# Last quarter of T4 split straight into its tile, the other three quarters loaded ahead

## Chip, cores and metric

The kernel runs on one core of one Trainium2 chip. The metric is the device time of one execution in microseconds (us); the median of several executions is compared. TensorE is called PE here, its weight loads PEld, VectorE DVE, ScalarE ACT, GpSimd POOL and SyncE SP. POOL and SP also issue DMA transfers, each from its own queue, in program order.

## What is computed

One inference step of a small encoder trunk with one layer: 2048 new frames of a first stream and 32 further frames of a running one, with 1024 channels. The part around the change is the combined input projection of the normed frames:

```python
def layer(h, p, conv_hist, pool_hist, pos, g_mix, w_in, ...):
    hn = rmsnorm(h, g_mix)
    proj = hn @ w_in                                    # (2048 + 32) x 1024 by 1024 x 3072
    hA, bA, cA, zA, vB, zB = jnp.split(proj, [W_A, 2 * W_A, 3 * W_A, 4 * W_A, 4 * W_A + W_B], axis=-1)
    yA, new_conv = short_conv_mixer(hA, bA, cA, zA, ...)
    yB, new_pool = pooling_mixer(vB, zB, ...)
    h = h + jnp.concatenate([yA, yB], axis=-1) @ w_out
    gate = jax.nn.sigmoid(rmsnorm(h, g_ple) @ w_ple_gate)
    return h + (p @ w_ple) * gate, new_conv, new_pool
```

A final RMSNorm closes the trunk. Everything is float32.

## The kernel before

**Products.** A float32 product is made of three passes: each operand is split into a high part (a cast, on ACT) and a low part (the rest, by a subtraction on DVE), and PE multiplies high by high, high by low and low by high. The helper `split` (L80) does both steps; `put` (L420) applies it to a whole piece of a tile. A half product, `half_product` (L642), is 12 matmuls of 128x128 by 128x512: four chunks of the inner size, three passes each.

**Seven instead of eight.** The 2048 frames are cut into blocks of 512 columns, and two blocks form a group (`GROUPS`). For a pair of weight columns and a pair of blocks, a 2x2 product of halves is made from seven half products (as Strassen and Winograd do) instead of eight. For that, seven combinations of the normed frames are needed, each split in two parts and kept in SBUF: 11, 21, T1, T2, T3, 22 and T4. For a group they fill three big slots of two pieces each, and T4 stands in a tile by itself from the pool `w7`, which has one buffer only (`seventh`, L366). `Unit.pair` (L970) makes the seven half products in a fixed order. Its last one, `half_product(X, make("22"), B["T4"], False)`, is the only one that reads T4; its result is the (1, 0) part.

**The first unit.** Group 0 begins with a unit done in plain form (`Unit.plain`, L902): eight half products for each of zb, v, c and h, first on block 0, then on block 1, without combinations. Block 1 is read from `hn[1]`, whose first half, `B0["12"]` (L774), lives in the one buffer of `w7`; the T4 of group 0 comes into the same buffer later. The last reader of `B0["12"]` is the product h of block 1. While the plain unit runs, the generator `second_block` (L777) prepares block 1 between its steps: it loads and norms the frames, turns them (on PE), splits them, and then makes the combinations T1, T2, T3 and T4 of group 0, for four column ranges of 128 (c = 0 to 3), one in each of its last four steps. T1, T2 and T3 are split straight into their pieces (L806 to L808). T4 can't be, since its buffer is still taken by `B0["12"]`: `to_memory` (L543) splits each quarter into a small tile of the pool `xin` (four buffers, shared with the raw frames) and writes it to `p_d["T4"]` in device memory, with a DMA from POOL's queue. After the product h, L940 and L941 allocate `B0["T4"]` and load all of it from memory with one DMA of 2 MB, again from POOL's queue; then the third pair of this unit, zab, goes on (`steps`), and its last half product reads T4. The fourth range (c = 3) is made in the step of `second` right after the product h of block 1, that is, just ahead of the load.

**What sets the order.** Tiles come from pools whose buffers are handed on when the last reader is done; a scheduler of the framework orders the instructions of each engine, and each engine then works in that order. A few instructions are pinned. A later unit's first matmuls, its weights' splits and the loads of its raw weights (`raw_weight`, L573, from SP's queue, ring `raws` of three buffers) are placed between those of the unit before.

Of the kernel before, what the change touches and what calls it, by code (L numbers as in the profile page):

```python
# [9 lines left out]
F32 = mybir.dt.float32  # L10
# [5 lines left out]
P = 128  # L16
# [20 lines left out]
def trunk(ctx, tc, x_p, x_s, c_conv, c_pool, p_p, p_s, g_mix, w_in, conv_w, conv_b, pool_w,  # L37
          pool_scale, w_out, g_ple, w_gate, w_ple, g_fin, y_p, y_s, sc_p, sp_p, sc_s, sp_s):
    nc = tc.nc
# [16 lines left out]
    def bank(name):  # L56
        return ps_m.tile([P, 512], F32, tag="mm", name=name)
# [22 lines left out]
    def split(hi, lo, src, eng=nc.vector, later=False):  # L80
        ins = nc.scalar.copy(hi, src)  # L81
        if later:
            tc.keep_in_program_order(ins)
        eng.tensor_tensor(lo, src, hi.bitcast(F32), op=ALU.subtract)  # L84
        return ins
# [256 lines left out]
    def plain(name, A, W, n, carry, out):  # L342

        X, Y, Z = (bank(f"{c}_{name}") for c in "xyz")
        packed(X, A[0], W["11"], n, True)
        c2 = carry(X, (0, 1))
        packed(Z, A[0], W["T1"], n, True)
        packed(Z, A[1], W["22"], n, False)
        out(Z, c2, (0, 1))
        packed(X, A[1], W["21"], n, False)  # L350
        out(X, None, (0, 0))
# [14 lines left out]
    def seventh(name):  # L366
        return w7.tile([P, 2 * KH * NH], F32R, tag="h", name=name)
# [31 lines left out]
    with ExitStack() as s1:  # L399
# [13 lines left out]
        def piece_of(t, i):  # L413

            return t[:, i * PIECE:(i + 1) * PIECE].rearrange("p (k h n) -> p k h n", k=KH, h=2)
# [4 lines left out]
        def put(piece, src, later=False):  # L420

            split(piece[:, :, 0], piece[:, :, 1], src, later=later)

        def ftile(name):
            return fr.tile([P, KH, P], F32, tag="f", name=name)
# [34 lines left out]
        def x_rows(tb, c):  # L460
            r = tb * NB + c * P
            return x_p[r:r + P]

        def x_load(name, src, queue=nc.sync):

            t, n = ring4(xin, f"xt_{name}"), src.shape[0]
            queue.dma_start(t[:n], src)
            return t, n, f"x{name}"

        def x_stat(x, later=False):  # L470

            t, n, name = x
            return t, n, sumsq(t, n, name, later=later)

        def normal(x):
            xt, n, r = x
            nc.vector.scalar_tensor_tensor(xt[:n], xt[:n], r[:n], g_bc[:n], op0=ALU.mult, op1=ALU.mult)

        def turn(x, half, name, get=tbank, later=False):
            xt, n, _ = x  # L480
            pt = get(name)
            for k in range(KH):
                kk = half * KH + k
                ins = nc.tensor.transpose(pt[:, k * P:k * P + n], xt[:n, kk * P:(kk + 1) * P], ident[:n, :n])
                if later:
                    tc.keep_in_program_order(ins)
            return pt.rearrange("p (k t) -> p k t", k=KH)[:, :, :n]
# [50 lines left out]
        p_d = {q: tc.dram_tile([P, KH, 2, NB], F32, name=f"p_d{q}") for q in NAMES}  # L538

        def staged(name):  # L540
            return xin.tile([P, KH, 2, P], F32R, tag="t", name=name)

        def to_memory(mem, name, src, at, later=False):  # L543
            t = staged(name)
            put(t, src, later)
            nc.gpsimd.dma_start(mem[:, :, :, at:at + P], t.bitcast(F32))
# [37 lines left out]
        def weights(kind, j, name):  # L584

            if first_w:
                return first_w.pop(0)
            raw = raw_weight(kind, j, name)
            out = []
            for half in range(2):  # L590
                out.append(wtile(f"w_{name}_{half}"))
                put(out[-1], raw[:, half * KH:half * KH + KH])
            return out
# [55 lines left out]
        def project(ps, w, tb):  # L649
            x = hn[tb]  # L650
            for half in range(2):
                half_product(ps, w[half], x[half], half == 0, half == 1)
# [36 lines left out]
        B0 = {}  # L689
# [87 lines left out]
        def second_block():  # L777

            spans = [(c, slice(c * P, c * P + P)) for c in range(4)]
            xs = []  # L780
            for c in range(4):
                x = x_stat(x_load(f"1_{c}", x_rows(1, c)))
                normal(x)
                xs.append(x)
                yield
            whole = []
            for c, cs in spans:
                x = xs[c]

                turned = x[0].rearrange("p (k t) -> p k t", k=KC)  # L790
                for half, q in enumerate(("12", "22")):
                    pt = turn(x, half, f"pt1_{c}_{half}", bank)
                    put(B0[q][:, :, :, cs], pt)
                    nc.scalar.copy(turned[:, half * KH:half * KH + KH], pt)
                whole.append((turned[:, :KH], turned[:, KH:]))
                yield
            op = lambda o, a, b, op=ALU.subtract: nc.vector.tensor_tensor(o, a, b, op=op)
            for c, cs in spans:
                p12, p22 = whole[c]
                t1, t3, t2, t4 = (ftile(f"f{t}_1_{c}") for t in range(4))  # L800
                part = lambda q, h: B0[q][:, :, h, cs].bitcast(F32)
                op(t1, p12, part("11", 0))
                op(t3, p22, p12)
                op(t1, t1, part("11", 1))
                op(t2, p22, t1)
                put(B0["T2"][:, :, :, cs], t2)  # L806
                put(B0["T1"][:, :, :, cs], t1)
                put(B0["T3"][:, :, :, cs], t3)  # L808
                op(t4, part("21", 0), t2)
                op(t4, t4, part("21", 1), ALU.add)  # L810
                to_memory(p_d["T4"], f"T4_0_{c}", t4, c * P)
                yield

        second = second_block()


# [19 lines left out]
        class Unit:  # L836
# [65 lines left out]
            def plain(self):  # L902
                tbs, j, tag, zs, V, U, c_s = self.tbs, self.j, self.tag, self.zs, self.V, self.U, self.c_s
                blocks = range(len(tbs))

                first = {}

                def product_of(kind, b, w):
                    if b == 0 and kind in first:
                        return first.pop(kind)  # L910
                    ps = bank(f"{kind}{tag}_{tbs[b]}")
                    project(ps, w, tbs[b])
                    return ps

                wz, wv = weights("zb", j, f"zb{tag}"), weights("v", j, f"v{tag}")
                wc = weights("c", j, f"c{tag}")
                first.update(first_products(dict(zb=wz, v=wv, c=wc)))
                for b in blocks:
                    nc.scalar.activation(self.cols(zs, b), product_of("zb", b, wz), AF.Silu)
                    ps = product_of("v", b, wv)  # L920
                    if b:
                        self.mix(0)
                        next(second)
                    nc.scalar.copy(self.place(V, HV, b), ps)
                    self.pool_block(b)
                    nc.scalar.copy(self.cols(c_s, b), product_of("c", b, wc))
                self.mix(1)
                next(second)

                nc.vector.tensor_copy(U[:, :HU], halo_u[:, :, j])  # L930
                wh = weights("h", j, f"h{tag}")
                for b in blocks:
                    ps = product_of("h", b, wh)
                    nc.vector.tensor_tensor(self.place(U, HU, b), ps, self.cols(c_s, b), op=ALU.mult)
                    self.conv(b)
                    if b == 0:
                        steps = self.pair(*self.third(B0), raw_ring, None, True)
                        next(steps)
                    next(second)
                B0["T4"] = piece_of(seventh("B0_T4"), 0)  # L940
                nc.gpsimd.dma_start(B0["T4"].bitcast(F32), p_d["T4"])  # L941
                p_d["T4"] = tc.dram_tile([P, KH, 2, NB], F32, name="p_dT4b")
                for _ in steps:
                    pass
# [356 lines left out]
    with ExitStack() as s2:  # L1301
# [160 lines left out]
        def short_tile():  # L1462
            plain("ol", short_a, W, last_n, *h_ops([short_x], last_n, "ol", two=True))
# [378 lines left out]
```

## Time and profile before

| what | us |
|---|---|
| time, median of 3 runs | 919.31 |
| lowest and highest of them | 918.29, 919.38 |
| time of the profiled execution | 917.26 |
| its span, from the first to the last instruction | 915.5 |

| engine in the profiled execution | busy us | share of the span |
|---|---|---|
| PEld | 722.7 | 79% |
| DVE | 702.6 | 77% |
| ACT | 460.3 | 50% |
| POOL | 151.6 | 17% |

The span is what the trace shows; 1.76 us of the profiled execution's own time lie around it. The plain unit and the pair zab that follows it lie in the first tenth of the span. The page's granted clock of PE is full throughout (0.999 on the mean). In a row of a timeline stand the start, the time from the start to the end, the engine, the line, the operation with out<-in, the shape and the count; in brackets, the idle time ahead of it and what ended it. Several equal instructions that follow each other make one row. In the profile's rows buffer numbers and digits are left out: `B_T` is T4's tile, `p_dT` the memory of a T combination (T4's, in the rows shown here), `T` one of the small tiles, `B` any piece of a big slot or the buffer of `B0["12"]`.

### The profile page before, as it was taken

What the parts mean: (1) busy time and instruction counts of PE and PEld (TensorE: products, weight loads), DVE (VectorE), ACT (ScalarE), POOL (GpSimd) and SP (SyncE); (2) the same over time, 40 slices, a digit from 0 to 9 for tenths busy, and PEclk for the clock granted to TensorE, in tenths of its full rate; (3) what the DMA queues carried; (4) which work ended last, traced back from release to release, by engine and by line L of the source; (5) the groups of instructions that cost most, each with busy time, mean ns of one, the idle gap of its engine ahead of it and who ended that gap; (6) DMA issues with size and microseconds to landing.
All of it is one profiled execution on the core that took longest, in us unless ns stands there. A gap on an engine that the chain in (4) does not pass through costs nothing.

```text
span 915.5 us, 12179 instructions
## 1 busy us (share of the span) xinstructions
PE 895.3 (98%) x4174; PEld 722.7 (79%) x4174; DVE 702.6 (77%) x1158; ACT 460.3 (50%) x834; POOL 151.6 (17%) x291
## 2 busy tenths in 40 slices
PE   8999999999999999999999999999999999999996
PEld 6787888878888877877778887888888788778885
DVE  6897899697894597856667679965576978897885
ACT  7743555555444344533344366544344865565554
POOL 2210121222122104100000020121111211120002
PEclk9999999999999999999999999999999999999999
DMA  8165386749499857577746485787677875575554
GB/s 275 53 186 184 115 239 182 219 147 301 122 313 427 244 161 228 191 231 247 244 132 215 146 310 206 259 235 273 226 258 291 287 256 173 184 234 187 183 187 171
DMA packets 113307, 199.56 MB, mean 218 GB/s; under 512 B 13190, under 2 KB 70062, under 8 KB 112221
## 3 DMA queue, kind: packets, MB, share of 16 engines
q1 hardware_dynamic: 91309, 124.72, 42.3%
q0 software_dynamic: 19488, 69.67, 22.5%
q10 hardware_dynamic: 2448, 4.39, 1.3%
q8 instruction: 33, 0.54, 0.2%
q14 instruction: 29, 0.24, 0.1%
HBM read 133.06 MB, written 65.67 MB: 217 GB/s over the span
## 4 chain that ended last, share of the span: by engine, by line
PE 65%; DMA 7%; issue 5%; DVE 2%; ACT 1%; POOL 1%; SPq 0%; POOLq 0%; DVEq 0%; ACTq 0%
PE x_g L185 9%; PE x_o L185 9%; PE x_zab L646 5%; PE z_g L185 5%; PE e L109 4%; PE x_zbv L646 4%; PE x_ch L646 4%; PE z_o L185 4%; DMA raw_zab_0b<-in_w_in_dram 4%; PE z_zab L646 2%; PE y_g L185 2%; PE y_o L185 2%; PE z_ch L646 2%; PE z_zbv L646 2%; DMA B<-p_d 2%
## 5 line engine op out<-in xcount | busy, mean ns | idle before, releaser
L646 PE MATMUL x_zab<-B,w_zab_S 128*128 128x512 f32 x192 | 46.9, 392 | 0.6 <-ACT V L983 0.4
L185 PE MATMUL z_o<-wo,y_S 128*128 128x512 f32 x192 | 47.4, 389 | 0.0
L185 PE MATMUL z_g<-wg,g_S 128*128 128x512 f32 x192 | 46.8, 391 | 0.0
L646 PE MATMUL z_zab<-B,w_zab_S 128*128 128x512 f32 x192 | 46.7, 390 | 0.0
L185 PE MATMUL x_o<-wo_T,y_S 128*128 128x512 f32 x192 | 46.1, 389 | 0.0
L185 PE MATMUL x_o<-wo,y 128*128 128x512 f32 x192 | 45.2, 389 | 0.0
L646 PEld LDWEIGHTS x_zab<-B,w_zab_S 128*128 128x128 f32 x192 | 35.7, 188 | 9.6 <-ACT V L983 0.8
L185 PEld LDWEIGHTS x_o<-wo,y 128*128 128x128 f32 x192 | 36.1, 188 | 7.7
L646 PEld LDWEIGHTS z_zab<-B,w_zab_S 128*128 128x128 f32 x192 | 35.8, 188 | 7.8 <-DVE w_zab_S L84 0.3
L185 PEld LDWEIGHTS z_o<-wo,y_S 128*128 128x128 f32 x192 | 36.0, 188 | 7.5
L646 PE MATMUL x_ch<-B,w_ch_S 128*128 128x512 f32 x168 | 41.9, 392 | 0.0
L185 PEld LDWEIGHTS x_o<-wo_T,y_S 128*128 128x128 f32 x192 | 36.0, 188 | 7.4
L646 PE MATMUL z_ch<-B,w_ch_S 128*128 128x512 f32 x168 | 40.5, 390 | 1.4 <-ACT U L983 1.4
L185 PEld LDWEIGHTS z_g<-wg,g_S 128*128 128x128 f32 x192 | 35.8, 188 | 7.5 <-ACT c_g L1566 0.2
L646 PE MATMUL x_zbv<-B,w_zbv_S 128*128 128x512 f32 x168 | 40.8, 392 | 0.6 <-ACT zs L983 0.6
L646 PE MATMUL z_zbv<-B,w_zbv_S 128*128 128x512 f32 x168 | 40.4, 390 | 0.0
L646 PEld LDWEIGHTS z_ch<-B,w_ch_S 128*128 128x128 f32 x168 | 31.5, 188 | 8.3 <-ACT U L983 1.8
L646 PEld LDWEIGHTS x_zbv<-B,w_zbv_S 128*128 128x128 f32 x168 | 31.3, 188 | 8.3 <-ACT zs L983 1.0
L646 PEld LDWEIGHTS x_ch<-B,w_ch_S 128*128 128x128 f32 x168 | 31.3, 188 | 7.3 <-issue 0.4
L646 PEld LDWEIGHTS z_zbv<-B,w_zbv_S 128*128 128x128 f32 x168 | 31.5, 188 | 6.5
L81 ACT CAST y_S<-y_fS 128x512 fp32r<-128x512 f32 x28 | 17.0, 620 | 27.2 <-PE x_o L185 11.5
L1316 DVE TENSOR_TENSOR c_o<-x_o,x 128x512 f32<-128x512 f32 x14 | 9.7, 690 | 21.9 <-PE x_o L185 21.8
(550 smaller groups left out, 2289.4 us busy)
## 6 DMA issues: line engine op xcount, KB each, us to landing
wn<-in_w_in_dram SPq DMA_DIRECT2D x24, 512.0 KB, 5.3
p_dT<-T POOLq DMA_DIRECT2D x16, 512.0 KB, 5.4
y<-y_d SPq DMA_DIRECT2D x16, 512.0 KB, 6.5
e<-e_d SPq DMA_DIRECT2D x15, 512.0 KB, 4.5
x<-in_x_prompt_dram SPq DMA_DIRECT2D x14, 512.0 KB, 5.2
B<-p_d POOLq DMA_DIRECT2D x3, 2048.0 KB, 15.7
B<-p_dT POOLq DMA_DIRECT2D x3, 2048.0 KB, 21.6
h_d<-x SPq DMA_DIRECT2D x12, 512.0 KB, 7.2
```

Source lines behind the costliest of these rows:

```text
L81: ins = nc.scalar.copy(hi, src)
L109: nc.tensor.matmul(ps, pps[:, a, k], wp[k][b][:, cs], start=k + q == 0, stop=k == 1 and q == 2)
L185: nc.tensor.matmul(ps[:n], lhs[:, k, a, :n], w[b][:, k], start=start and k + q == 0, stop=k == KH - 1 and q == 2, skip_group_check=True)
L646: nc.tensor.matmul(ps, lhs[:, k, x], b[:, k, y], start=start and k + q == 0, stop=stop and k == KH - 1 and q == 2, skip_group_check=True)
L1316: add = lambda o, a, b: nc.vector.tensor_tensor(o, a, b, op=ALU.add)
```

## The change

Of the four quarters of T4 the first three are still split into small tiles and written to memory. In the step of the fourth, the tile `B0["T4"]` is allocated, one DMA loads the columns of the first three quarters from memory, and the fourth is split straight into its own columns of the tile. The allocation and the whole load after the product h are gone.

```diff
                 op(t4, part("21", 0), t2)
                 op(t4, t4, part("21", 1), ALU.add)
-                to_memory(p_d["T4"], f"T4_0_{c}", t4, c * P)
+                if c < 3:
+                    to_memory(p_d["T4"], f"T4_0_{c}", t4, c * P)
+                else:
+                    B0["T4"] = piece_of(seventh("B0_T4"), 0)
+                    nc.gpsimd.dma_start(B0["T4"][:, :, :, :c * P].bitcast(F32), p_d["T4"][:, :, :, :c * P])
+                    put(B0["T4"][:, :, :, cs], t4)
                 yield
...
                     next(second)
-                B0["T4"] = piece_of(seventh("B0_T4"), 0)
-                nc.gpsimd.dma_start(B0["T4"].bitcast(F32), p_d["T4"])
                 p_d["T4"] = tc.dram_tile([P, KH, 2, NB], F32, name="p_dT4b")
```

In the rows that follow, a name ends with its buffer's number, and digits inside are dropped: `B_T_807` and `B_T_803` are T4's tile, `T_0_0` to `T_0_3` the four small tiles, `p_dT_176` T4's memory. Lines of the changed kernel are up to five higher than before.

On POOL, around the writes of the four quarters, before (the names behind `waits` are counters: `DMASW0` to `DMASW3` count the landings of the four writes, in order):

```order
L546 DMA p_dT_176<-T_0_0_623 1024x1x128 [waits DVE_49]
L546 DMA p_dT_176<-T_0_1_684 1024x1x128 [waits DVE_49]
L546 DMA p_dT_176<-T_0_2_753 1024x1x128 [waits DVE_49]
L546 DMA p_dT_176<-T_0_3_803 1024x1x128 [waits DVE_49]
L941 DMA B_T_807<-p_dT_176 128x4096 [waits DMASW2_49,DMASW1_49,DMASW3_49,DMASW0_49,PE_49]
L73 TENSOR_SCALAR ms_x_3_976<-ssq_x_3_974 128x1 [waits Activation_49]
```

and with the change:

```order
L546 DMA p_dT_176<-T_0_0_623 1024x1x128 [waits DVE_49]
L546 DMA p_dT_176<-T_0_1_684 1024x1x128 [waits DVE_49]
L546 DMA p_dT_176<-T_0_2_753 1024x1x128 [waits DVE_49]
L815 DMA B_T_803<-p_dT_176 128x8x384 [waits DMASW1_49,DMASW2_49,DMASW0_49,PE_49]
L73 TENSOR_SCALAR ms_x_3_974<-ssq_x_3_972 128x1 [waits Activation_49]
```

The fourth write is gone, and the load waits for the three others and for PE (the last matmul that reads `B0["12"]`). It moves 8 runs of 384 elements in each partition where it moved one run of 4096.

On PE, where the pair zab ends and the next unit's first pair, zbv, begins, before (`x_`, `y_` and `z_` are the three accumulators of a pair):

```order
L646 MATMUL x_zab_0_810<-B_2_187,w_zab_0_S_876 128x512 x12
L646 MATMUL z_zab_0_812<-B_2_187,w_zab_0_S_893 128x512 x12
L646 MATMUL x_zbv_1_951<-B_0_185,w_zbv_1_11_954 128x512 x2
L646 MATMUL x_zab_0_810<-B_T_807,w_zab_0_22_913 128x512 x12
L646 MATMUL x_zbv_1_951<-B_0_185,w_zbv_1_11_954 128x512 x10
L646 MATMUL y_zbv_1_952<-B_0_185,w_zbv_1_12_986 128x512 x12
```

and with the change:

```order
L646 MATMUL x_zab_0_808<-B_2_187,w_zab_0_S_874 128x512 x12
L646 MATMUL z_zab_0_810<-B_2_187,w_zab_0_S_891 128x512 x12
L646 MATMUL x_zab_0_808<-B_T_803,w_zab_0_22_911 128x512 x12
L646 MATMUL x_zbv_1_949<-B_0_185,w_zbv_1_11_952 128x512 x12
L646 MATMUL y_zbv_1_950<-B_0_185,w_zbv_1_12_984 128x512 x12
```

Two matmuls of zbv that stood ahead of T4's twelve now stand behind them. It is the only place where PE's order differs.

On ACT, at the cast of the fourth quarter, before:

```order
L81 COPY w_zab_0_S_844<-raw_zab_0a 128x4x128 [waits DVE_49]
L81 COPY w_zab_0_S_860<-s_zab_0_726 128x4x128
L81 COPY T_0_3_803<-f_1_3_790 128x4x128 [waits DMASW1_49,DVE_49]
L983 COPY V_0_334<-x_zab_0_810 128x512 [waits PE_49]
L81 COPY w_zab_0_S_876<-raw_zab_0b 128x4x128 [waits DMAHW5_49]
```

and with the change:

```order
L81 COPY w_zab_0_S_842<-raw_zab_0a 128x4x128 [waits DVE_49]
L81 COPY w_zab_0_S_858<-s_zab_0_726 128x4x128
L81 COPY B_T_803<-f_1_3_790 128x4x128 [waits DVE_49,PE_49]
L986 COPY V_0_334<-x_zab_0_808 128x512 [waits PE_49]
L81 COPY w_zab_0_S_874<-raw_zab_0b 128x4x128 [waits DMAHW5_49]
```

The cast keeps its place; it writes into T4's tile, waits for PE (again the last reader of `B0["12"]`) where it waited for an earlier write's landing, and does not wait for the load. DVE's subtraction for the same quarter keeps its place too. SP's order is unchanged.

## Prediction

> **What bounds the kernel now.** I began with the page's busy times.
>
> ```profile
> span 915.5 us, 12179 instructions
> PE 895.3 (98%) x4174; PEld 722.7 (79%) x4174; DVE 702.6 (77%) x1158; ACT 460.3 (50%) x834; POOL 151.6 (17%) x291
> ```
>
> PE is busy for 895.3 of 915.5 us, so an edit that adds or takes no matmul can win only from the 20.2 us in which PE stands still. Next I read the list of waits, for PE alone over the whole span, because it names these gaps (total us, times, longest).
>
> ```profile
> PE x_zab L646 <- DMA B_T<-p_dT: 2.3, 1, 2.3
> PE e L109 <- DMA wq<-wl_d: 1.6, 1, 1.6
> PE z_ch L646 <- ACT U L983: 1.4, 1, 1.4
> ```
>
> The first is the load that the change touches: once, for 2.3 us. PE's timeline shows the place.
>
> ```profile
> 57.87 11.04 PE L646 MATMUL h<-B,w_h 128*128 128x512 f32 x48
> 82.50 2.88 PE L646 MATMUL z_zab<-B,w_zab_S 128*128 128x512 f32 x12
> 85.22 0.61 PE L646 MATMUL x_zbv<-B,w_zbv 128*128 128x512 f32 x2
> 88.11 2.98 PE L646 MATMUL x_zab<-B_T,w_zab 128*128 128x512 f32 x12 [2.28 <-DMA B_T<-p_dT]
> 90.94 2.43 PE L646 MATMUL x_zbv<-B,w_zbv 128*128 128x512 f32 x10
> 93.20 2.88 PE L646 MATMUL y_zbv<-B,w_zbv 128*128 128x512 f32 x12
> 95.92 2.88 PE L646 MATMUL x_zbv<-B,w_zbv_S 128*128 128x512 f32 x12
> ```
>
> Starts tell the pace: y_zbv begins at 93.20 and the next twelve at 95.92, so twelve matmuls take 2.72 us and one takes 0.227. PE was free for T4's product at 85.22, bridged 0.45 us with two matmuls of the next pair, and stood until 88.11. Why was the load late? POOL's timeline has the writes of the third and fourth quarter and the load, and the DMA part of the trace gives the times from issue to landing (for the stretch from 45 to 95 us, except the last row, which is from the whole span).
>
> ```profile
> 63.36 0.85 POOL L546 DMA_DIRECT2D p_dT<-T  x1 [10.17 <-DVE T L84]
> 73.90 0.85 POOL L546 DMA_DIRECT2D p_dT<-T  x1 [9.69 <-DVE T L84]
> 78.27 0.57 POOL L941 DMA_DIRECT2D B_T<-p_dT  x1 [3.52 <-PE x_zab L646]
> p_dT<-T POOLq DMA_DIRECT2D x4, 512.0 KB, 4.4
> DMA to landing us min/median/max: 3.8/4.4/5.6
> B_T<-p_dT POOLq DMA_DIRECT2D x1, 2048.0 KB, 9.7
> raw_zbv_1a<-in_w_in_dram SPq DMA_DIRECT2D x1, 512.0 KB, 3.8
> raw_ch_1b<-in_w_in_dram SPq DMA_DIRECT2D x1, 512.0 KB, 10.6
> B_T<-p_dT4b POOLq DMA_DIRECT2D x1, 2048.0 KB, 29.3
> ```
>
> The fourth write is issued at 73.90; 78.27 - 73.90 = 4.37 us later, the time of such a write to land, POOL issues the load, and 78.27 + 9.7 = 88.0 is when PE goes on. (The row names PE as releaser; the matmul that the load needs was long done, as worked out below, so it was the write.) The chain is: fourth quarter's split, write, whole load, PE.
>
> **The change, part by part.**
>
> *The load ahead.* It needs three landed writes and the last reader of the buffer. The third write is issued at 63.36; with the 3.8 to 5.6 us that such writes take it has landed between 67.2 and 69.0. The last reader is in the h row: its 48 matmuls start at 57.87, the first 24 belong to block 0, and the next 12 read the buffer, so the 36th ends by 57.87 + 36 x 0.227 + 0.4 = 66.4. The writes end last: issue at up to 69.0. What do the transfer engines do then?
>
> ```profile
> 64.00:68.00 4.00, 4.00 (x19) 3.34 (x18) 4.00 (x8) 1.12 (x2) 0.21 (x1) 1.00 0.83 253
> 68.00:72.00 4.00, 4.00 (x20) 3.23 (x19) 4.00 (x9) 2.10 (x4) 0.00 (x0) 1.00 0.03 9
> 72.00:76.00 4.00, 4.00 (x19) 3.10 (x18) 4.00 (x8) 1.27 (x3) 0.85 (x1) 1.00 0.18 53
> 76.00:80.00 4.00, 4.00 (x19) 3.31 (x18) 4.00 (x9) 3.31 (x7) 0.57 (x1) 1.00 0.46 129
> 80.00:84.00 4.00, 4.00 (x19) 3.33 (x18) 3.95 (x7) 1.81 (x3) 0.00 (x0) 1.00 1.08 406
> 84.00:88.00 4.00, 1.84 (x9) 1.18 (x7) 0.27 (x1) 0.62 (x1) 0.00 (x0) 1.00 1.00 359
> 104.00:108.00 4.00, 4.00 (x24) 3.39 (x22) 2.92 (x6) 1.90 (x4) 0.00 (x0) 1.00 0.00 0
> ```
>
> The columns are the stretch, its length, busy time of PE, PEld, DVE, ACT and POOL with counts, the granted clock, the DMA share and GB/s. From 68 to 76 the engines idle (9 and 53 GB/s, and the latter is mostly the write that goes away), while from 80 to 88, where the load runs now, they are full. The new load moves three quarters of the bytes in shorter runs, a shape that the trace does not show. Its cost is bounded by the nearest rows: below by one load of 512 KB, 3.8 us; above by three quarters of the slowest load of a T4 tile, 0.75 x 29.3 = 22 us. I take three quarters of the same load now, 0.75 x 9.7 = 7.3, because that row shares the buffer and the queue, and it was measured on fuller engines. The load then lands at 69.0 + 7.3 = 76.3, where PE asks at 85.22: 8.9 us to spare. Even three loads of 512 KB at the writes' median, 13.2 us, would land at 82.2.
>
> *PE.* T4's twelve now follow at once, then the other pair's twelve: 85.22 + 2 x 2.72 = 90.66 for the start of y_zbv, where it was 93.20. **The term is -2.54 us**; it holds the gap of 2.28 and some 0.26 of restart. PE's other needs at 85.22 are met: DVE, in its order, has finished all that the product reads before the row at 83.59 below.
>
> *The fourth quarter.* Its cast and subtraction change only their target: nothing on ACT's or DVE's time. The cast gets a wait for PE, and behind it stand on ACT the copy of x_zab's accumulator, for which PE waits, and the next weights.
>
> ```profile
> 71.66 0.61 ACT L81 CAST T<-f 128x512 fp32r<-128x512 f32 x1
> 92.47 0.63 ACT L954 ACTIVATE V<-V 128x512 f32<-128x512 f32 x1 [6.38 <-DVE V L986]
> 93.52 0.58 ACT L983 COPY zs<-x_zbv 128x512 f32<-128x512 f32 x1
> 79.67 0.47 SPq L578 DMA_DIRECT2D raw_ch_1b<-in_w_in_dram  x1
> 83.59 0.68 DVE L84 TENSOR_TENSOR w_zbv_S<-s_zbv,w_zbv_S 128x512 fp32r<-128x512 f32 x1
> 90.41 0.69 DVE L618 TENSOR_TENSOR s_ch<-raw_ch_1b 128x512 f32<-128x512 f32 x1 [6.14 <-DMA raw_ch_1b<-in_w_in_dram]
> 91.75 0.68 DVE L986 TENSOR_TENSOR V<-z_zab,V 128x512 f32<-128x512 f32 x1
> 104.29 0.69 DVE L986 TENSOR_TENSOR V<-x_zbv,V 128x512 f32<-128x512 f32 x1 [0.71 <-PE x_zbv L646]
> ```
>
> The cast runs at 71.66 and its new wait ends by 66.4: nothing, with 5.3 us of cover.
>
> *What was hidden, and is late next.* DVE stands from 84.27 to 90.41 for raw_ch_1b, a raw weight that SP issues at 79.67 into the same crowd: 10.6 us to land, where raw_zbv_1a took 3.8. DVE's wait holds up V<-z_zab, that holds up ACT's silu at 92.47, and behind this, at 93.52, ACT copies x_zbv's accumulator, which PE needs to go on with x_zbv. Today that costs nothing, as the copy ends at 94.1 and PE comes at 95.92. With the change PE comes at 95.92 - 2.54 = 93.38. If raw_ch_1b landed as late as now, PE would wait 0.7 us. But the 2 MB are out of its way: with 3.8 us, or the 5.6 of the slowest write, it lands at 83.5 to 85.3, so about 5 us earlier, and 0.7 us earlier would do. I take nothing, and keep 0.7 for the range.
>
> *Traffic and memory.* One write of 512 KB and a quarter of the load fall away. One small tile fewer moves the ring of `xin` by one place, so some waits name a neighbour's transfer; around 70 us those are writes that have landed by then, and I count nothing.
>
> *After that.* By 104.29 DVE waits for PE again, and from 104 to 108 nothing moves on the DMA engines: whatever was late has been caught up, so everything behind should follow PE, earlier by the same 2.54. The next gap of PE is short.
>
> ```profile
> 140.97 1.06 ACT L94 ACTIVATE junk<-xt 128x1024 bf16<-128x1024 f32 x1 [2.05 <-DMA xt<-in_x_prompt_dram]
> 143.17 3.02 PE L646 MATMUL x_zab<-B,w_zab_S 128*128 128x512 f32 x12 [0.42 <-ACT V L983]
> ```
>
> There ACT waits 2.05 us for frames, and PE for ACT. These loads are released by work that PE paces, so I let the gap stand.
>
> *Sum.* 915.5 - 2.54 = 912.96 for the span, 917.26 - 2.54 = 914.72 for the profiled execution's own time. The median of the runs shown is 2.05 above that execution, so for it 919.31 - 2.54 = **916.8 us**. A measurement of this kernel tells apart about 0.2%, which is 1.84 us.
>
> [...]
>
> **The rivals.**
>
> *A, gain eaten (no change).* Either raw_ch_1b stays late: then 2.54 - 0.7 = 1.84 is left, 917.5. Or later gaps grow, since a load that does not come earlier with PE (the frames at 140.97 are one) gives back what PE gained, up to all of it: 919.3. For it: ACT waits for frames several times. Against it: the idle engines at 104 to 108.
>
> *B, the load ahead is late (slower).* It would sit on POOL's queue or run slowly in its short runs, and PE, which has no two matmuls to bridge with any more, waits for it at 85.22. The new y_zbv starts 5.44 us after the load's landing, against 93.20: it breaks even at 87.8 and costs over 1.84 us from 89.6 on, thus from 20.6 us after an issue at 69.0. At the upper bound of 22 us it lands at 91.0, y_zbv starts at 96.4, 3.2 us later than now: 922.5. [...] For it: B_T<-p_dT4b did take 29.3. Against it: that load was one of seven in a row, this one meets empty engines.
>
> *C, more than the gap.* DVE is 5 us earlier from 84 on, so writes and loads behind it spread, and the gap of 0.42 at 143.17 and half of the 1.4 before z_ch go too: 919.31 - 2.54 - 1.1 = 915.7.
>
> **How the numbers follow.** The forecast as summed gets 0.60, C 0.12, A 0.18, B 0.10. Faster is forecast and C, 0.72; within 0.2% is A, 0.18; slower is B, 0.10. The range reaches below C by the scatter of the runs (about 1 us between 918.29 and 919.38): 914.7; above it takes in A to its end, 919.3. It leaves out B. The likeliest case alone has 916.1 to 917.5.
>
> **What would show it.** Right: PE's row of x_zab<-B_T starts at about 85.2 without a wait; the load is issued at 67 to 69 and lands before 80; DVE's wait for raw_ch_1b is below 2 us; y_zbv starts at 90.7; and PE's busy time is unchanged while its list of waits has lost the first row. The step on the load is wrong if PE still waits there; the step on what is late next, if x_zbv<-B waits for ACT near 93.4; and the step that all behind follows, if the gaps at 143 or 188 have grown by what was won.

## The result, and the profile after

The changed kernel takes 915.72 us (median of 20 runs, 913.53 to 918.41), the kernel before beside it 919.7 (915.68 to 924.4). The ratio is 0.9954, with a 95% interval of 0.9941 to 0.9968: faster by 4.2 us, between 2.9 and 5.4. The forecast was 916.8 by a gain of 2.54 us. The time lies in the range, faster was the likeliest sign, and the gain is larger than its one term; why, is the question of the experiments.

The profiled execution of the changed kernel took 916.19 us, its span is 914.4. PE is busy for 895.2 us (895.3 before). From the list of PE's waits over the whole span (total us, times, longest):

```profile
PE gm L447 <- DMA gm_row<-in_g_mix_dram: 2.3, 1, 2.3
PE e L109 <- DMA wq<-wl_d: 1.5, 2, 0.9
PE z_ch L646 <- ACT U L986: 1.1, 1, 1.1
PE x_zbv L646 <- ACT zs L986: 0.8, 1, 0.8
PE x_zbv L646 <- DVE V L989: 0.7, 1, 0.7
PE x_zab L646 <- ACT V L986: 0.5, 1, 0.5
```

The row of T4's load is gone. Of the rows shown that of 0.7 us for `V` is new; the others were there before within 0.3 us. The timelines of four engines around T4, in the changed kernel:

```profile
57.54 11.04 PE L646 MATMUL h<-B,w_h 128*128 128x512 f32 x48
84.91 2.88 PE L646 MATMUL x_zab<-B_T,w_zab 128*128 128x512 f32 x12
87.63 2.88 PE L646 MATMUL x_zbv<-B,w_zbv 128*128 128x512 f32 x12
90.35 2.88 PE L646 MATMUL y_zbv<-B,w_zbv 128*128 128x512 f32 x12
93.07 2.88 PE L646 MATMUL x_zbv<-B,w_zbv_S 128*128 128x512 f32 x12
67.93 0.92 POOL L815 DMA_DIRECT2D B_T<-p_dT  x1 [4.05 <-DMA p_dT<-T]
85.61 0.69 DVE L618 TENSOR_TENSOR s_ch<-raw_ch_1b 128x512 f32<-128x512 f32 x1 [1.67 <-DMA raw_ch_1b<-in_w_in_dram]
90.55 0.59 ACT L986 COPY zs<-x_zbv 128x512 f32<-128x512 f32 x1 [1.74 <-PE x_zbv L646]
```

T4's twelve start at 84.91 with no wait, and y_zbv, the mark of the prediction, at 90.35 where it was 93.20. That is 2.85 us; but the whole stretch runs 0.33 us earlier in this execution (h starts at 57.54, before at 57.87). From the start of h to that of y_zbv it was 93.20 - 57.87 = 35.33 us and is 90.35 - 57.54 = 32.81: **2.52 us less**, and the forecast's term was 2.54. DVE's wait for raw_ch_1b fell from 6.14 to 1.67, and ACT's copy of x_zbv's accumulator now waits for PE instead of DVE: it ends at 91.14, well before PE comes at 93.07. The landing times, from the DMA part of the trace for 45 to 100 us (count, KB, median us from issue to landing):

```profile
B_T<-p_dT POOLq DMA_DIRECT2D x1, 1536.0 KB, 7.7
raw_ch_1b<-in_w_in_dram SPq DMA_DIRECT2D x1, 512.0 KB, 6.1
```

So near T4 the trace shows what was forecast, and 2.5 us of gain. The two profiled executions, though, are only 1.1 us apart (917.26 and 916.19), while the medians are 4.0 apart. One execution of the kernel before does not tell where its median is.

### The profile page after: what moved, and what is told of

It is laid out like the page before. It is cut to its first block, busy times and chain, and to the rows that moved or that the text cites. A ratio compares the mean times of both kernels' runs of the same rounds, so it can differ in the third digit from the quotient of the medians.

```text
span 914.4 us, 12174 instructions
## 1 busy us (share of the span) xinstructions
PE 895.2 (98%) x4174; PEld 722.6 (79%) x4174; DVE 702.6 (77%) x1158; ACT 460.8 (50%) x834; POOL 149.9 (16%) x290
## 4 chain that ended last, share of the span: by engine, by line
PE 51%; issue 12%; DMA 10%; DVE 3%; POOL 1%; ACT 1%; SPq 0%; POOLq 0%; ACTq 0%; DVEq 0%
PE x_g L185 9%; PE x_o L185 8%; PE z_g L185 5%; PE z_o L185 4%; DMA raw_zab_0b<-in_w_in_dram 4%; PE x_ch L646 3%; PE x_zbv L646 3%; PE x_zab L646 2%; PE y_g L185 2%; PE e L109 2%; PE y_o L185 2%; DMA B<-p_d 2%; PE z_ch L646 1%; PE new L1152 1%; PE z_zab L646 1%
```

## The experiments

### Both kernels again, unchanged

Two theories stood here. G: the length of T4's gap changes from execution to execution, and the profiled one had a short gap. C is the prediction's rival of that letter: the change takes more than the gap, in later waits. The kernel before was profiled three more times, the changed one once more, all on one chip; the expectations call these further profiles the looks.

> The kernel before, unchanged. Theory G (the gap): the measured gain, about 4 us in the medians, is PE's wait for T4's load, and the profiled execution happened to have a short one (2.3 us). Then looks at the kernel before show this wait at different lengths, 2 to 7 us, about 4 us on the mean, and spans that differ by about as much as the waits do. Theory C (the crowd): the wait is always near 2.3 us, and the rest of the gain comes from what the crowd of transfers at 78 to 90 us does elsewhere. Then the waits agree within 0.5 us, and spans above 915.5 are longer at other places.

> The kernel before, unchanged, once more. G: the wait for T4's load between 2 and 7 us, and the span moves with it. C: the wait within 0.5 us of 2.3, and spans move for other reasons.

> The kernel before, unchanged, a third time. G: as in the other looks, the wait and the span move together. C: the wait stays near 2.3 us.

> The changed kernel, unchanged. Both theories: no wait for T4's load, x_zab<-B_T starts within 0.5 us of 85. G: the span lies 2 to 5 us below those of the looks at the kernel before, by what they waited. C: the row of x_zab<-B_T is 2.5 us earlier, and the difference in the spans comes about after 110 us.

They took 922.13, 918.29, 918.73 and 917.98 us. The wait for T4 hardly moves. What moves is the time of the twelve matmuls behind it. PE's timeline in the first further profile of the kernel before:

```profile
87.91 4.57 PE L646 MATMUL x_zab<-B_T,w_zab 128*128 128x512 f32 x12 [2.26 <-DMA B_T<-p_dT]
92.32 2.44 PE L646 MATMUL x_zbv<-B,w_zbv 128*128 128x512 f32 x10
94.60 2.88 PE L646 MATMUL y_zbv<-B,w_zbv 128*128 128x512 f32 x12
```

4.57 us where the first profile had 2.98. The reason stands in the view of windows (stretch, length, busy time of PE, PEld, DVE, ACT and POOL with counts, granted clock, DMA share, GB/s) of the same execution:

```profile
84.00:88.00 4.00, 1.74 (x9) 1.15 (x8) 0.07 (x1) 0.62 (x1) 0.00 (x0) 1.00 1.00 353
88.00:89.00 1.00, 1.00 (x3) 0.80 (x4) 0.00 (x0) 0.00 (x0) 0.00 (x0) 0.55 1.10 356
89.00:90.00 1.00, 1.00 (x3) 0.73 (x3) 0.00 (x0) 0.00 (x0) 0.00 (x0) 0.50 0.17 59
90.00:91.00 1.00, 1.00 (x4) 0.79 (x3) 0.87 (x2) 0.00 (x0) 0.00 (x0) 0.50 0.01 2
91.00:92.00 1.00, 1.00 (x5) 0.83 (x4) 1.00 (x2) 0.00 (x0) 0.00 (x0) 0.75 0.36 137
92.00:93.00 1.00, 1.00 (x6) 0.80 (x5) 0.90 (x3) 0.85 (x2) 0.00 (x0) 1.00 0.98 365
```

The granted clock falls to 0.50 just after PE has gone on and comes back some 3.4 us later. The means of single microseconds tell when: 0.55, 0.51 and 0.85 from 88 to 89 in the three further profiles put the fall 0.2 to 0.6 us after PE's restart (87.91, 87.79, 88.12), and 0.75 and 0.78 from 91 to 92 in the first two, 0.95 from 92 to 93 in the third, the return. In the view above the row from 89, at half clock, counts three matmuls in its microsecond, the last row six. In the first profile the same stretch was at 1.00 throughout; its row for the microsecond from 89:

```profile
89.00:90.00 1.00, 1.00 (x6) 0.83 (x5) 0.00 (x0) 0.00 (x0) 0.00 (x0) 1.00 0.19 68
```

All executions so far, in us:

| execution | h starts | wait for T4 | T4's twelve | y_zbv starts | from h to y_zbv |
|---|---|---|---|---|---|
| before, first profile | 57.87 | 2.28 | 2.98 | 93.20 | 35.33 |
| before, three further profiles | 57.67, 57.65, 57.78 | 2.26, 2.17, 2.34 | 4.57, 4.58, 4.58 | 94.60, 94.50, 94.81 | 36.93, 36.85, 37.03 |
| after, first profile | 57.54 | none | 2.88 | 90.35 | 32.81 |
| after, further profile | 57.90 | none | 2.88 | 90.70 | 32.80 |

G falls, as the gap is constant. A new theory, K, takes its place: the gap costs its 2.5 us, and in three of the four profiles a further 36.94 - 35.33 = 1.6 us for the half clock behind it, together 36.94 - 32.81 = 4.1, inside the interval of the measured gain. Between the third further profile of the kernel before and that of the changed one, starts on PE differ by 4.11 us at y_zbv, 4.01 at 190 us and 3.95 at 560, so what is won at T4 is kept up to there. By these profiles C is not needed.

The further profiles also show a scatter of both kernels far behind T4: near 670 us, in the output projection, PE sometimes waits for DVE's `c_o` (2.24 us in the first further profile of the kernel before, 0.31 in the second, none in the third, 1.95 in that of the changed kernel; none there in the first profile of either). The clock does there what it did at T4: the twelve matmuls behind the 1.95 took 4.52 us, at a granted clock of 0.69 on the mean from 668 to 672 us. The changed kernel's further profile lost there most of what it had won.

### Keep PE busy in the gap, change nothing else

The kernel before, with 24 transposes on PE ahead of T4's product, into a bank that nobody reads:

```diff
-                half_product(X, make("22"), B["T4"], False)
+                w22 = make("22")
+                if self.gi + self.j == 0:
+                    fill(24, tbank("warm"))
+                half_product(X, w22, B["T4"], False)
```

> The kernel before, with 24 transposes of the identity on PE (about 0.1 us each, results unused) between the last product ahead of T4's and T4's own, so that PE has work for about 2.4 us while it waits for the load. Theory K (clock): the wait costs twice, about 2.5 us as time and about 1.6 us more in most executions, because PE gets half its clock for some 3.5 us behind a gap of over 2 us. Then the granted clock is 1.00 from 88 to 92 us, T4's twelve take 2.9 to 3.1 us (4.6 in the looks), y_zbv starts near 93.3 (94.5 to 94.8 in the looks), and the median is 0.8 to 1.8 us below before. Rival S: T4's matmuls are slow because of the crowd of transfers or of their freshly landed operand. Then they take 4.6 us here too, and the time is that of before or longer.

916.13 us (915.46 to 918.96); ratio to the kernel before 0.9965, interval 0.9952 to 0.9978. PE's timeline:

```profile
88.31 2.99 PE L646 MATMUL x_zab<-B_T,w_zab 128*128 128x512 f32 x12 [0.48 <-DMA B_T<-p_dT]
93.85 2.88 PE L646 MATMUL y_zbv<-B,w_zbv 128*128 128x512 f32 x12
```

The load is as late as ever (the product starts at 88.31), yet the twelve take 2.99 us, at a clock of 1.00 through the whole stretch:

```profile
89.00:90.00 1.00, 1.00 (x7) 0.78 (x5) 0.00 (x0) 0.00 (x0) 0.00 (x0) 1.00 0.13 45
```

The second kernel with the transposes, further below, agrees: T4's twelve in 3.00 us at a clock of 1.00. Two executions are few, as the clock held without transposes too, behind the 2.28 us of the first profile. But over all profiles of this document the line is clear: where PE's waits between 84 and 96 us were at most 1.39 us long the clock never fell there (eight executions), and where PE waited 1.96 us or more for T4 it fell in four of six. So in these runs the fall went with PE's idle time, and not with the load, which is as late with the transposes, nor with what else was being moved (the DMA share from 84 to 88 us was 1.01 there and 0.98 to 1.00 in the further profiles): K, as far as the clock goes.

From h (57.70) to y_zbv it is 36.15 us, 0.8 better than in the further profiles; of the 1.6 us of half clock the other half is lost again, as the product starts 0.4 us later after h and the two matmuls that bridged the gap now come behind it. The median's gain of 3.2 us (2.0 to 4.4) lies outside the 0.8 to 1.8 that K gave. At the first matmul into y_o, near 558 us, this execution is still only 0.5 to 0.8 us ahead of the three further profiles, and 1.0 behind the first; the rest came about behind that, in part near 670 us, where it had no wait. Whether the transposes have to do with that, one profile can't tell. It stays open, and with it how much of the 4.2 us that the change gained in the medians is T4's: the traces show 2.5 us in the first pair, and 4.1 where the clock fell.

### One half of the change at a time

First only the load ahead: three quarters are loaded ahead as in the change, but the fourth still goes through memory, with a write and a load of 512 KB of its own.

```diff
                     nc.gpsimd.dma_start(B0["T4"][:, :, :, :c * P].bitcast(F32), p_d["T4"][:, :, :, :c * P])
-                    put(B0["T4"][:, :, :, cs], t4)
+                    to_memory(p_d["T4"], f"T4_0_{c}", t4, c * P)
+                    nc.gpsimd.dma_start(B0["T4"][:, :, :, cs].bitcast(F32), p_d["T4"][:, :, :, cs])
```

> The changed kernel, but the fourth quarter goes through memory again: split into a small tile, written, and loaded by a DMA of its own (512 KB); the three others are loaded ahead as in the change. It tells whether the load ahead or the direct split carries the gain. Load ahead: the write is issued near 74 and lands near 78, the small load lands at 82 to 86, PE waits for at most 1 us, the clock stays at 1.00, and the time is 3 to 4.5 us below before (ratio 0.995 to 0.997). Direct split: the small load gets into the crowd as the large one did and lands at 87 or later, PE waits for 2 us or more with the clock halved, ratio 0.999 to 1.001.

921.1 us (916.47 to 923.72); ratio 1.0017, interval 1.0002 to 1.0033: not faster than the kernel before. Its timelines of POOL and PE:

```profile
69.37 0.92 POOL L815 DMA_DIRECT2D B_T<-p_dT  x1 [5.40 <-DMA p_dT<-T]
73.66 0.85 POOL L546 DMA_DIRECT2D p_dT<-T  x1 [3.37 <-DVE T L84]
80.20 0.90 POOL L817 DMA_DIRECT2D B_T<-p_dT  x1 [5.68 <-DMA p_dT<-T]
88.10 4.38 PE L646 MATMUL x_zab<-B_T,w_zab 128*128 128x512 f32 x12 [2.95 <-DMA B_T<-p_dT]
```

The fourth write is issued at 73.66, about as before, but it runs beside the load of the other three and has landed only 80.20 - 73.66 = 6.5 us later (4.37 in the kernel before). Its small load takes 7.8 us in the crowd after 80. PE waits 2.95 us and then runs at half clock (0.50 from 90 to 92). Write and load take 6.5 + 7.8 = 14.3 us, where they took 4.37 + 9.7 = 14.1. What the small load saved, 1.9 us, the write lost again beside the load ahead, 2.2. (PE's wait is longer than before also because no two matmuls bridge it now.) What a small last load is worth without that collision, no run shows.

Then only the direct split: the fourth quarter goes straight into the tile, but the three quarters are loaded as late as the whole was, held back by a wait for a cast on ACT, the `last_cast` when the load is written down.

```diff
                     B0["T4"] = piece_of(seventh("B0_T4"), 0)
-                    nc.gpsimd.dma_start(B0["T4"][:, :, :, :c * P].bitcast(F32), p_d["T4"][:, :, :, :c * P])
                     put(B0["T4"][:, :, :, cs], t4)
...
+                for _ in range(6):
+                    next(steps)
+                load = nc.gpsimd.dma_start(B0["T4"][:, :, :, :3 * P].bitcast(F32), p_d["T4"][:, :, :, :3 * P])
+                tc.add_manual_dep(load.ins, last_cast[0].ins.name, ...)
```

> The changed kernel, but the load of the three quarters is held back until a cast on ACT that ends near 77.5 us, about where the load of before was issued; the fourth quarter is split straight into the tile. If the load ahead carries the gain: 1.5 MB in the crowd land at 85 to 87.5, PE waits 0.2 to 2.3 us; with a wait above about 2 us the clock is halved behind it. Ratio 0.997 to 1.000, and by theory K the row of T4's twelve is slow if and only if the wait was long. If the direct split carries it: no wait at all, ratio 0.995 to 0.996.

916.58 us (915.54 to 917.81); ratio 0.9971, interval 0.9961 to 0.9982. Its timelines of POOL, PE and DVE:

```profile
77.30 0.92 POOL L948 DMA_DIRECT2D B_T<-p_dT  x1 [13.35 <-ACT w_zab_S L81]
86.13 3.00 PE L648 MATMUL x_zab<-B_T,w_zab 128*128 128x512 f32 x12 [1.02 <-DMA B_T<-p_dT]
91.69 2.88 PE L648 MATMUL y_zbv<-B,w_zbv 128*128 128x512 f32 x12
88.69 0.69 DVE L620 TENSOR_TENSOR s_ch<-raw_ch_1b 128x512 f32<-128x512 f32 x1 [4.68 <-DMA raw_ch_1b<-in_w_in_dram]
```

Issued 0.97 us earlier than the whole load was and a microsecond shorter (8.7 against 9.7), the load leaves a wait of 1.02 us, and behind that the clock holds (1.00 in every window from 84 to 93 us): 3.00 us for the twelve. From h (57.61) to y_zbv it is 34.08, which is 2.9 less than in the further profiles, and the median gained 2.7 (1.7 to 3.6). By the medians the direct split alone carries about two thirds of the gain; as the intervals overlap, and as 0.97 us of the shorter wait are the earlier issue, the share is not exact. It pays twice here: the gap is 1.02 us where it was 2.17 to 2.34, and behind it the clock held. The expectation had put this wait and this ratio down to a load ahead that carries the gain; but the load ahead gained nothing by itself, so the halves do not simply add up. It pays once the fourth quarter needs no write: from h to y_zbv the changed kernel takes 32.81, and this one 34.08.

### Put the crowd back

The changed kernel with 2 MB of idle traffic, a copy within device memory on POOL's queue that nothing waits for, at the place where the whole load used to run:

```diff
+                for _ in range(6):
+                    next(steps)
+                load = nc.gpsimd.dma_start(tc.dram_tile([P, 4 * D], F32, name="aside"), x_p[:4 * P].rearrange("(p r) d -> p (r d)", r=4))
+                tc.add_manual_dep(load.ins, last_cast[0].ins.name, ...)
```

> The changed kernel with an idle copy of 2 MB from memory to memory put on POOL's queue near 77.5 us, where the load of before stood; nothing waits for it. It gives DVE its late raw weight back. Theory K: no wait for T4, raw_ch_1b lands at 88 to 91, PE waits up to 0.9 us for ACT's copy of x_zbv's accumulator near 93.4 and nothing else, so the time is 0 to 1 us above the changed kernel (ratio to before 0.995 to 0.997). Theory C (the crowd): what the crowd did to DVE and the transfers behind it was a good part of the gain; then 1.5 us or more of it is lost (ratio 0.997 or above).

917.6 us (916.41 to 920.35); ratio 0.9986, interval 0.9972 to 0.9999. Its timelines of POOL, SP, DVE, ACT and PE:

```profile
77.20 0.54 POOL L949 DMA_DIRECT2D aside<-in_x_prompt_dram  x1 [8.84 <-ACT w_zab_S L81]
79.32 5.76 SPq L580 DMA_DIRECT2D raw_ch_1b<-in_w_in_dram  x1
90.87 0.69 DVE L620 TENSOR_TENSOR s_ch<-raw_ch_1b 128x512 f32<-128x512 f32 x1 [6.96 <-DMA raw_ch_1b<-in_w_in_dram]
93.97 0.57 ACT L993 COPY zs<-x_zbv 128x512 f32<-128x512 f32 x1
94.60 3.01 PE L648 MATMUL x_zbv<-B,w_zbv_S 128*128 128x512 f32 x12 [1.39 <-ACT zs L993]
```

There is no wait for T4, but SP needs 5.76 us to issue raw_ch_1b (0.39 in the changed kernel), it lands 11.4 us after that issue began, DVE stands for 6.96 us, ACT's copy comes at 93.97, and PE waits for it: rival A's chain, link by link. It costs 94.60 - 93.07 = 1.53 us against the changed kernel. So rival A was a real danger: with 2 MB in the stretch in which raw_ch_1b is loaded, a part of what the change wins is lost. The copy is not the load, though: it is issued 1.07 us earlier and goes from memory to memory, so the size of the loss is the copy's own. By the numbers (1.5 us or more lost, a ratio of at least 0.997) this is the case that the expectation gave to C. The trace tells the two apart: in the kernel before, ACT's copy was nearly as late (93.52) and cost nothing, since PE came at 95.92. So the crowd held back PE's later work only once the gap was gone, and its removal is no part of the 2.5 us. The clock holds at 1.00 behind this wait of 1.39 us (94 to 96), and behind one of 1.99 us for `c_o` near 668 us (668 to 676), the scatter that comes next.

### The scatter near 670 us

What makes PE wait for `c_o` is seen on ACT. Its timeline in the first further profile of the kernel before, with POOL's row ahead and PE's behind:

```profile
655.19 1.34 POOL L1370 DMA_DIRECT2D gs<-in_w_ple_gate_dram  x2 [11.97 <-DMA g_d<-gs]
657.83 0.60 ACT L81 CAST y_S<-y_fS 128x512 fp32r<-128x512 f32 x1
664.54 0.72 ACT L1376 ACTIVATE gs<-gs,vec 128x512 f32<-128x512 f32 x1 [6.11 <-issue]
666.95 0.72 ACT L1376 ACTIVATE gs<-gs,vec 128x512 f32<-128x512 f32 x1 [1.69 <-DMA gs<-in_w_ple_gate_dram]
668.36 1.14 ACT L81 CAST y_S<-y_fS 128x512 fp32r<-128x512 f32 x2 [0.68 <-PE y_o L185]
670.44 4.29 PE L185 MATMUL z_o<-wo,y_S 128*128 128x512 f32 x12 [2.24 <-DVE c_o L1316]
```

ACT scales rows of the gate weight (`gs`) in between; they come by loads from POOL's queue, which wait for the store of the rows ahead (`g_d`). ACT stands for 6.11 us ahead of the first scaling (the row names no transfer) and for 1.69 ahead of the second (it names the load), and the splits of y_S stand behind both. Theory S: this chain makes the scatter. To take it off ACT, scaling and stores were moved to POOL in three kernels: the one before, the changed one, and the one with the transposes.

```diff
-                    ins = nc.scalar.activation(t, t, AF.Copy, scale=vec[:, 100 + k:101 + k])
+                    ins = nc.gpsimd.tensor_scalar(t, t, scalar1=vec[:, 100 + k:101 + k], scalar2=None, op0=ALU.mult)
...
-                    nc.scalar.dma_start(g_d[k * P:k * P + P, half * NH:half * NH + NH], t)
+                    nc.gpsimd.dma_start(g_d[k * P:k * P + P, half * NH:half * NH + NH], t)
```

> The kernel before, with one thing changed far behind T4: the scaling of the gate weight's rows (gs, 16 instructions of 128x512) and its stores go from ACT to POOL. Theory S (the scatter near 655-672): ACT works in order, its scaling waits up to 6.1 us for a load of 256 KB that POOL issues, the splits of y_S stand behind it, so PE waits for c_o (0 to 2.2 us in the looks, and up to 3.8 with the half clock behind it). By S no wait of PE for c_o over 0.5 us near 660-697 is left, and the median is 0.5 to 2.0 us below the kernel before. T4's own wait stays at 2.2-2.3 us, with the half clock behind it in most executions (x_zab<-B_T row about 4.57). Rival: the gap there is another transfer's, then PE still waits for c_o and the median stays; second rival: POOL, blocked behind its own loads, is late with the norm factors rs_h, and the time rises by over 2 us.

> The changed kernel with the same move of the gate weight's scaling to POOL. If the scatter near 655-672 is the same in both kernels and the change acts only at T4, this one stands to before_pool as the change to the kernel before: theory K (gap 2.5 and half clock 1.6 us, of which some is given back) says 3 to 4.2 us less than before_pool; the prediction's own term says 2.5; the median against the kernel before is then 3.5 to 6 us lower (ratio 0.9935 to 0.996). If the gain of 4.2 held a part of luck with the scatter, the difference between the two pool kernels is nearer to 2.5. PE has no wait for T4.

> warm_gap (24 transposes in PE's gap ahead of T4's product) with the same move of the gate weight's scaling to POOL. Theory K: the clock stays at 1.00 behind the gap, the x_zab<-B_T row takes 3.0 us, and without the scatter the difference to before_pool is what was seen at y_zbv, 0.6 to 1.6 us, not the 3.2 of warm_gap's median; then 3.2 was part luck with the scatter. If the difference to before_pool is 3 us again, the transposes or the clock save more than the row near T4 shows, and something behind it is to be looked for.

| kernel | median (range), us | ratio to the kernel before, interval |
|---|---|---|
| kernel before, scaling on POOL | 929.18 (928.32 to 933.45) | 1.011, 1.0082 to 1.0138 |
| changed kernel, scaling on POOL | 925.02 (916.67 to 930.65) | 1.0039, 1.0015 to 1.0064 |
| transposes, scaling on POOL | 923.91 (916.9 to 930.98) | 1.003, 1.0001 to 1.0059 |

As S says, none of the three profiles has a wait of PE for `c_o`; but five of the ten profiles with the scaling at its old place have none near 670 us either, so this supports S and does not show it. And all three kernels became slower, where S gave a gain; in the profiles that is near 714 us. PE's timeline of the kernel before with the scaling on POOL, and then SP's:

```profile
714.01 0.49 PE L109 MATMUL e<-wq,pps 128*128 128x512 f32 x1 [3.25 <-DMA wq<-wl_d]
716.98 1.22 PE L109 MATMUL e<-wq,pps 128*128 128x512 f32 x2 [2.47 <-DMA wq<-wl_d]
692.53 15.07 SPq L1387 DMA_DIRECT2D wg_b<-g_d  x4
707.71 3.50 SPq L1519 DMA_DIRECT2D wq<-wl_d  x4
```

SP's loads of the scaled rows back from memory (`wg_b`) need the stores, the last of which POOL issues at 704.12 (in the profile of the changed kernel ACT issues it at 690.11). They take 15.07 us to be issued (3.73 in that profile), and the loads of wq behind them on SP go out at 707.71 instead of 700.93. PE waits four times, 7.8 us in all, and the granted clock is 0.50 from 716 to 724 us. The second rival had named POOL as the one to fall behind, but through the norm factors; it was through its stores. The changed kernel lies 4.2 us below the one before in this pair too, and the one with the transposes 5.3, more than either case of its expectation; but the runs of both spread over 14 us, so that says little.

This execution of the kernel before adds a row to the table of T4: a wait of 1.96 us, and twelve matmuls in 2.97 us, at full clock.

The last run went the other way about it: the changed kernel with its eight scalings laid at other steps of the output projection, all but the last one earlier, and further apart.

```diff
-        GATE_STEPS = (2, 5), (4, 3), (6, 1), (6, 6), (8, 4), (10, 2), (12, 1), (12, 5)
+        GATE_STEPS = (2, 1), (2, 6), (4, 5), (6, 3), (8, 2), (10, 1), (10, 6), (12, 5)
```

> The changed kernel with the eight scalings of the gate weight's rows laid at other steps of the output projection: they start earlier and stand five or six of its steps apart (now five, five, five, five, five, six and four). The scaling stays on ACT, its loads on POOL. Theory S (the scatter near 655-672 is a chain load, scaling, store, next load that needs some 13 us where the steps give 13.5): with more room ACT's scaling waits less, PE has no wait for c_o over 0.5 us, and the median lies 0.5 to 1.5 us below the changed kernel: ratio to the kernel before 0.993 to 0.995. Rival: the chain is slowed by the traffic at that place, the frames' loads and the stores of h, whatever its steps; then the wait for c_o comes in some executions as before, and the ratio is that of the changed kernel, 0.994 to 0.997. PE has no wait for T4 in either case.

915.81 us (913.44 to 920.8); ratio 0.9964, interval 0.9945 to 0.9983, the same as the changed kernel. ACT's and PE's timelines:

```profile
610.91 0.72 ACT L1379 ACTIVATE gs<-gs,vec 128x512 f32<-128x512 f32 x1 [5.06 <-DMA gs<-in_w_ple_gate_dram]
656.29 0.72 ACT L1379 ACTIVATE gs<-gs,vec 128x512 f32<-128x512 f32 x1
618.51 3.02 PE L185 MATMUL x_o<-wo_T,y_S 128*128 128x512 f32 x12 [1.09 <-DVE c_o L1319]
```

At 656 there is no wait; at 611 one of 5.06 us has come, and PE waits 1.09 us for `c_o` at 618.51. S had no wait over 0.5 us, and a median below the changed kernel's; both failed, and the rival's ratio came out. In this one profile the wait moved rather than went. No run gave a version that beats the changed kernel.

## Why the prediction was right, and where its size was off

- **The bound**: right. PE's busy time is the same within 0.1 us in both kernels, and the time came out of one of its gaps.
- **The load ahead**: right. Issued at 67.93 (at most 69.0 was forecast), landed 7.7 us later (7.3 taken), so at 75.6, 9.3 us ahead of PE (8.9). The rival of a late load is out.
- **The term of -2.54 us**: right for what it counts, 2.52 on the trace. It was too small for the kernel's time, and this is the step that was off. It took "some 0.26 of restart" from one execution, in which the clock had held; in three of four profiles of the unchanged kernel (three of five with the one that has its scaling on POOL) the restart costs 1.6 us more, at half clock. A gap of 2.5 us is then one of 4.1, and with three of five 3.5 on the mean, both inside the measured 2.9 to 5.4. The sum also carried the 2.05 us by which the median lay above that execution over to the changed kernel whole, though a half clock behind the gap is a part of such a difference that the change takes away. The profile's row of the clock could not warn of it: it is of one execution. That row is not quite full, either: the clock falls 5.0 us after PE's last matmul, at the end of the span, where nothing waits for PE.
- **The cast on ACT, and what is late next**: right. DVE waits 1.67 us for raw_ch_1b ("below 2"), and the copy is in time, though raw_ch_1b took 6.1 us to land where at most 5.6 were taken. The price of a late raw_ch_1b, 0.7 us, was too low: put back, it cost 1.5, since raw_ch_1b came 0.46 us later still than in the kernel before, and the stretch ran a little earlier.
- **That all behind follows**: in the main. The gap near 143 us stayed (0.42, now 0.45) and that near 188 shrank by 0.2 (1.35, now 1.11). A wait of 0.69 us for `V` at 230.55 is new in the profiled pair, but it is not the change's: the changed kernel's further profile has none, and the kernel before with its scaling on POOL has one of 0.64. What hid the gain in that pair is the other execution: the first profile of the kernel before had neither the half clock nor the wait for `c_o`, and its 917.26 us lay below the median of 919.7.
- **The rivals**: A's chain exists, but its condition is gone with the 2 MB. C's time, 915.7, is the measured one, by luck: the waits that it named did not shrink by 1.1 us (z_ch 1.35 to 1.11, the other 0.42 to 0.45); what came on top of the gap was, as far as the traces show it, the clock.

## What to carry to other kernels

Here a wait of PE, the engine that bounds the kernel, had a price beyond its length: behind 2.17 to 2.34 us the next twelve matmuls took 4.57 or 4.58 us in three of four profiles, and 2.98 in the other. So read the granted clock of the microseconds behind the gap, in more than one execution, before the gap is priced. Where the last piece of a load makes a round trip through memory, look whether it can be taken off the trip: here that took the write's landing, 4.37 us, off the chain, while loading the rest ahead of a piece that still made the trip gained nothing, as the write then took 6.5 us beside the load ahead. And before a waiting instruction is moved to an idle engine, look at the loads and stores that hang on it there: with the scaling on POOL, SP's loads of its rows took 15.07 us to be issued instead of 3.73.

## What the runs showed of the hardware

First, stops of PE of some 2 us already stood ahead of a fall of its clock, but not always. Of the waits for T4, ACT's copy and `c_o` above, those of 1.02 and 1.39 us did not cost it, nor did the one before z_ch near 188 us, 0.99 to 1.70 us in every execution (its twelve took 3.02 to 3.04); of those from 1.95 to 2.34 five did (1.95, 2.17, 2.24, 2.26, 2.34) and three did not (1.96, 1.99, 2.28); the one of 2.95 did. Shorter ones, close together, had a fall among them: in the profile of the changed kernel with its scaling on POOL the clock fell at 712.1 us, behind waits of 0.57 and 1.33 us and inside one of 1.07.

```profile
709.30 0.49 PE L109 MATMUL e<-wq,pps 128*128 128x512 f32 x1 [0.57 <-DMA wq<-wl_d]
711.13 0.74 PE L109 MATMUL e<-wq,pps 128*128 128x512 f32 x2 [1.33 <-DMA wq<-wl_d]
712.93 0.79 PE L109 MATMUL e<-wq,pps 128*128 128x512 f32 x1 [1.07 <-DMA wq<-wl_d]
```

At the end of the span, where PE has no more to do, the clock fell 5.0 us after PE's last matmul in the first profile of the kernel before (907.76 to about 912.75) and 1.9 us after it in that of the changed kernel (906.68 to about 908.6). At T4 it fell 0.2 to 0.6 us after PE had gone back to work, and returned some 3.4 us later, and the twelve matmuls took 4.57 or 4.58 us instead of 2.98.

Second, a write of 512 KB landed in 4.37 us on nearly idle transfer engines (53 GB/s from 72 to 76 us, the write's own share included) and in 6.5 beside a load of 1.5 MB, and one and the same load of 512 KB, raw_ch_1b, in 6.1 us behind the change and in 11.4 beside the copy of 2 MB: 1.5 and 1.9 times as long.
